# Half of a convolution's taps from VectorE to ScalarE products and GpSimd sums

## The chip, the cores and the metric

The kernel runs on one core of a Trainium2 chip. The core has five engines that work side by side, each with a queue of its own that it takes strictly in order: TensorE (PE in the profile: matrix multiplications, with PEld for the loads of their weights), VectorE (DVE), ScalarE (ACT), GpSimd (POOL) and SyncE (SP, which issues DMAs). An instruction that waits for another engine holds up everything behind it in its own queue. The metric is the device time of one execution in microseconds (us); a comparison is made with the median of several runs.

## The reference, cut to what matters

The program computes three blocks of a network on 512 positions of 1024 features. The change lies in the second block. There a projection of the normalised input yields, among other things, two groups of 1024 columns, `a` and `b`. They make a gated linear unit, and a causal convolution of width 31 runs over the positions, for each feature with its own 31 weights:

```
glu[t, f] = a[t, f] * sigmoid(b[t, f])
z[t, f]   = conv_b[f] + sum over j = 0..30 of conv_w[j, f] * glu[t - 30 + j, f]
z         = layernorm(z) over the features, then silu, times a sigmoid gate
```

In the same block runs a recurrent layer (`rwkv`) over 16 heads. Its state steps depend on each other, chunk after chunk of 64 positions.

## The kernel before, in words

Activations lie with features on the partitions: 1024 features are eight tiles of 128 partitions by 512 positions. Matrix products are made with operands that are split into a high and a low part (three matmuls at L123, L124 and L125 for one product; the text calls these the large matmuls). The weights come by DMA in slabs; ScalarE casts a slab's high part (`whi`, L117) and another engine subtracts to get the low part (`wlo`, L118). In the block in question two slabs of three leave that subtraction to GpSimd (`lo_on = "vpp"`, L1007). The results of the large matmuls lie in four PSUM banks, `psg` (pool `pg`, L37), which are handed out in the order in which the program asks for them: an output that needs a bank waits until whoever reads the bank's earlier content has done so.

The recurrent layer is worked through in eight pairs of heads, 0 to 7. For each pair there are three parts. `rwkv_prep` (L1040) projects to `k`, `r` and `v` by large matmuls of 384 columns, normalises (`ps_kn`, L1086; GpSimd multiplies `kk` at L1104), makes the products `ps_M` (L1117), and writes a piece of them to memory and back in another layout. `rwkv_invert` (L1149) inverts small triangular blocks on VectorE: L1177 is its first instruction, the reductions at L1172 its last; the result goes through memory, and TensorE transposes it (`ps_D`, L1211). `rwkv_steps` (L1232) then makes the eight chunk steps: per chunk TensorE, VectorE (`zV` L1251, `S` L1261) and ScalarE (`zV` L1252, `VU` L1256) hand over to each other several times, and at the end a normalised `Y` is transposed (`ps_yt`, L1281).

The loop at the end of `block2` records, for each pair p, the steps of p, the preparation and inversion of p + 1, and then filler work from the list `order`: `c12` are convolution tiles 1 and 2, `g02` two gate tiles from 0, and so on ("c01", "c12", "c31 g02", "c42", "g22", "c62 g41", ...). Fillers have a lower priority (`fill_offset`). A scheduler puts all of it into the engines' queues when the program is built. What the order in a queue becomes depends on what it expects of each engine.

`conv_tiles` (L1289) makes one convolution tile i: large matmuls for `b` and `a`, ScalarE's sigmoid into `glu` (L1298), VectorE's product with `a` (L1301), ScalarE's tap 0 with the bias into `z[i]` (L1303), and then 30 taps on VectorE, each `z = glu shifted * weight + z` in one instruction (L1305). The first of them is kept behind the last instruction of the inversion that was recorded before (`issue_after`, L1308). GpSimd adds the tile to a running sum `zs` (L1312, L1314). `gate_tiles` (L1322) reads a gate's PSUM bank by a sigmoid into a tile `gs` (L1327) and sends it to memory. That tile comes from the ring `tmp`, which has three buffers:

```
    def tmp(self, name, parts=128):
        return self.sp.tile([parts, T], F32, tag="tmp", name=name, bufs=3)
```

## Time and profile before

| what | value |
|---|---|
| median of 3 runs | 3337.91 us (3335.11 to 3338.43) |
| profiled execution, its own time | 3332.78 us |
| its span in the profile | 3331.0 us |
| granted TensorE clock, mean | 0.983 |
| busy: PE, DVE, ACT, POOL | 95%, 61%, 42%, 15% of the span |
| 240 taps at L1305 | 197.0 us busy, from 1411.2 to 1921.7 us |

A busy TensorE is not TensorE at its peak: matmuls are pipelined and their ends are modelled. Busy shares over the whole program mix stages with different limits, so the stage of the taps has to be read alone. In that stage the text uses the first `ps_D` transpose of each pair as a mark, D0 to D7 for pairs 0 to 7.

### The profile page before, as it was taken

How to read it: one execution, taken by the hardware profiler on the slowest of the kernel's cores; microseconds unless marked ns; L12 is line 12 of the kernel's file. 1: busy time of each engine (PE TensorE's matmuls, PEld its weight loads, DVE VectorE, ACT ScalarE, POOL GpSimd, SP SyncE). 2: the span in 40 equal slices, each digit the busy share in tenths (PEclk: the TensorE clock that was granted, in tenths of full speed). 3: DMA queues.
4: the chain of work that ended last, by engine and by line, in shares of the span. 5: the costliest groups of instructions: out<-in, count | busy, mean ns of one | idle time of the engine just before them, and what ended most of it. 6: DMA issues, size and time to landing. Idle time of an engine off the chain costs nothing. (4 is left out here: it accounts for less than half of the span.)

```text
span 3331.0 us, 43197 instructions
## 1 busy us (share of the span) xinstructions
PE 3179.2 (95%) x15337; PEld 2471.1 (74%) x15337; DVE 2041.3 (61%) x4002; ACT 1386.5 (42%) x2784; POOL 515.1 (15%) x603
## 2 busy tenths in 40 slices
PE   8999999999999999898899889999999999999998
PEld 6755778788778887666666656788877777788887
DVE  4576764654665356688778875434367764575665
ACT  3466332333443233454444444433244553343444
POOL 1000010111211011222223323111010011110111
PEclk9999999999999999999999999999999999999999
DMA  4411553525223332322122343233233125332322
GB/s 134 120 62 50 172 169 128 176 97 149 68 83 95 100 97 76 103 63 68 52 68 66 101 134 113 85 96 95 95 92 112 55 84 164 110 95 95 95 95 82
DMA packets 275032, 332.60 MB, mean 100 GB/s; under 512 B 52956, under 2 KB 188058, under 8 KB 274817
## 3 DMA queue, kind: packets, MB, share of 16 engines
q1 hardware_dynamic: 237392, 301.43, 29.4%
q10 hardware_dynamic: 33489, 12.39, 1.5%
q0 software_dynamic: 3936, 16.03, 1.5%
q8 instruction: 121, 1.98, 0.2%
q14 instruction: 94, 0.77, 0.1%
HBM read 311.88 MB, written 23.89 MB: 101 GB/s over the span
## 5 line engine op out<-in xcount | busy, mean ns | idle before, releaser
L118 DVE TENSOR_TENSOR wlo<-raw,whi 128x512 fp32r<-128x512 f32 (+2 forms) x865 | 625.2, 734 | 752.7 <-PE psg L124 419.3
L123 PE MATMUL psg<-hhi,whi 128*128 128x512 f32 (+1 forms) x2624 | 1044.5, 401 | 36.4 <-DVE glu L1301 7.0
L125 PE MATMUL psg<-hhi,wlo 128*128 128x512 f32 (+1 forms) x2624 | 1038.9, 397 | 13.3 <-DVE wlo L118 7.9
L124 PE MATMUL psg<-hlo,whi 128*128 128x512 f32 (+1 forms) x2624 | 1041.2, 397 | 0.0
L117 ACT CAST whi<-raw 128x512 fp32r<-128x512 f32 (+2 forms) x975 | 581.7, 604 | 1072.6 <-PE psg L124 924.6
L123 PEld LDWEIGHTS psg<-hhi,whi 128*128 128x128 f32 (+1 forms) x2624 | 496.5, 189 | 162.8 <-issue 17.2
L125 PEld LDWEIGHTS psg<-hhi,wlo 128*128 128x128 f32 (+1 forms) x2624 | 496.7, 189 | 124.9 <-POOL wlo L118 9.6
L124 PEld LDWEIGHTS psg<-hlo,whi 128*128 128x128 f32 (+1 forms) x2624 | 497.1, 189 | 107.2 <-issue 7.6
L123 PE MATMUL psg<-hidhi,whi 128*128 128x512 f32 x784 | 308.4, 394 | 1.0 <-DVE ffu L574 0.8
L125 PE MATMUL psg<-hidhi,wlo 128*128 128x512 f32 x784 | 308.0, 393 | 0.0
L124 PE MATMUL psg<-hidlo,whi 128*128 128x512 f32 x784 | 305.9, 390 | 0.0
L1305 DVE SCALAR_TENSOR_TENSOR z<-glu,par_B,z 128x512 f32<-128x512 f32 x240 | 197.0, 835 | 1.5
L118 POOL TENSOR_TENSOR wlo<-raw,whi 128x512 fp32r<-128x512 f32 (+1 forms) x110 | 146.8, 1341 | 281.3 <-ACT whi L117 217.3
L125 PEld LDWEIGHTS psg<-hidhi,wlo 128*128 128x128 f32 x784 | 147.2, 188 | 34.0
L124 PEld LDWEIGHTS psg<-hidlo,whi 128*128 128x128 f32 x784 | 147.2, 188 | 33.4
L123 PEld LDWEIGHTS psg<-hidhi,whi 128*128 128x128 f32 x784 | 147.4, 188 | 32.8 <-DVE ffu L574 1.3
L581 POOL TENSOR_TENSOR ffu<-ffu,ffg 128x512 f32<-128x512 f32 x44 | 64.7, 1469 | 582.6 <-DVE ffu L574 582.6
L1374 POOL TENSOR_TENSOR ffr<-ffr 128x512 f32<-128x512 f32 x32 | 40.1, 1261 | 293.0 <-ACT ffr L1373 286.9
L194 ACT CAST hidhi<-ffu 128x512 fp32r<-128x512 f32 x66 | 41.0, 622 | 106.1 <-POOL ffu L581 66.2
L195 DVE TENSOR_TENSOR hidlo<-ffu,hidhi 128x512 fp32r<-128x512 f32 x66 | 57.3, 868 | 30.9 <-ACT hidhi L194 29.4
L765 DVE SCALAR_TENSOR_TENSOR adacc<-adraw,c_act,adacc 128x1024 f32<-128x1024 f32 x42 | 53.9, 1284 | 33.4 <-DMA adraw<-in_ada_w_dram 33.0
L209 POOL TENSOR_TENSOR ss<-ss,sq 128x512 f32<-128x512 f32 x24 | 35.2, 1467 | 218.1 <-ACT sq L208 202.0
(572 smaller groups left out, 4040.3 us busy)
## 6 DMA issues: line engine op xcount, KB each, us to landing
raw<-in_ffn_w_gu_dram SPq DMA_DIRECT2D x176, 256.0 KB
raw<-in_w_in_dram SPq DMA_DIRECT2D x59, 512.0 KB
adraw<-in_ada_w_dram SPq DMA_DIRECT2D x48, 512.0 KB
raw<-in_w_up_dram SPq DMA_DIRECT2D x88, 256.0 KB
raw<-in_ffn_w_down_dram SPq DMA_DIRECT2D x42, 512.0 KB
raw<-in_w_ff_in_dram SPq DMA_DIRECT2D x32, 512.0 KB
raw<-in_w_ff_out_dram SPq DMA_DIRECT2D x32, 512.0 KB
raw<-in_w_in_dram SPq DMA_DIRECT2D x96, 128.0 KB
```

The costliest lines, as they stand in the source:

```text
L117: nc.scalar.copy(oi(hi), ri(r))
L118: eng.tensor_tensor(out=oi(lo), in0=ri(r), in1=fr(oi(hi)), op=ALU.subtract)
L123: first = nc.tensor.matmul(ps, lhsT=whi, rhs=xhi, start=start, stop=False)
L124: nc.tensor.matmul(ps, lhsT=whi, rhs=xlo, start=False, stop=False)
L125: nc.tensor.matmul(ps, lhsT=wlo, rhs=xhi, start=False, stop=stop)
L194: nc.scalar.copy(hi, t)
L195: nc.vector.tensor_tensor(out=lo, in0=t, in1=fr(hi), op=ALU.subtract)
L209: (nc.gpsimd if c < 4 else nc.vector).tensor_tensor(out=ss, in0=ss, in1=sq, op=ALU.add)
L581: nc.gpsimd.tensor_tensor(out=t, in0=t, in1=part[c], op=ALU.mult)
L765: nc.vector.scalar_tensor_tensor(out=acc, in0=raw, scalar=c[:, k:k + 1], in1=acc, op0=ALU.mult, op1=ALU.add)
L1305: tap = nc.vector.scalar_tensor_tensor(out=z[i], in0=g[:, j:j + T], scalar=cw(j), in1=z[i], op0=ALU.mult, op1=ALU.add)
L1374: nc.gpsimd.tensor_tensor(out=t, in0=t, in1=t, op=ALU.mult)
```

## The change

For the odd tiles (1, 3, 5 and 7) each of the 30 taps becomes two instructions: ScalarE writes `glu` shifted, times the weight, into a new tile of the ring `tmp`, and GpSimd adds that tile to `z[i]`. The even tiles stay as they are. The branch leaves the loop body by `continue`, so for an odd tile nothing is kept behind the inversion.

```diff
             for j in range(1, 31):
+                if i % 2:
+                    pr = self.tmp("tap")
+                    nc.scalar.activation(out=pr, in_=g[:, j:j + T], func=AF.Copy, scale=cw(j))
+                    nc.gpsimd.tensor_tensor(out=z[i], in0=z[i], in1=pr, op=ALU.add)
+                    continue
                 tap = nc.vector.scalar_tensor_tensor(out=z[i], in0=g[:, j:j + T], scalar=cw(j), in1=z[i],
                                                      op0=ALU.mult, op1=ALU.add)
```

Lines behind it move by five: the taps of the even tiles are L1310, the gates L1332. The scheduler now puts the queues together in another order. Three places of it follow, all around tile 3 and the steps of pair 2. In the rows `psg` are the outputs of large matmuls, numbers tell buffers of one name apart.

TensorE before, from the `ps_D` transposes of pair 2 (D2):

```order
L1211 MATMUL ps_D_12768<-ident_81,zD0_10970 128x128 x4
L124 MATMUL psg_13563<-hlo5_10792,whi_13642 128x512
L125 MATMUL psg_13563<-hhi5_10791,wlo_13643 128x512
L123 MATMUL psg_13564<-hhi4_10785,whi_13638 128x512
L1217 MATMUL ps_T_12775<-D_12773,zC_10964 32x32 x16
L124 MATMUL psg_13564<-hlo4_10786,whi_13638 128x512
L125 MATMUL psg_13564<-hhi4_10785,wlo_13639 128x512
L123 MATMUL psg_13564<-hhi5_10791,whi_13642 128x512
L124 MATMUL psg_13564<-hlo5_10792,whi_13642 128x512
L125 MATMUL psg_13564<-hhi5_10791,wlo_13643 128x512
```

TensorE in the change, from the same transposes:

```order
L1211 MATMUL ps_D_12828<-ident_81,zD0_10970 128x128 x4
L1217 MATMUL ps_T_12835<-D_12833,zC_10964 32x32 x16
L1225 MATMUL ps_X_12854<-zD0_10970,zT_10965 32x32 x16
L1253 MATMUL ps_y_13121<-S_13117,ar_12705 64x128
L1255 MATMUL ps_u_13130<-zV0_10968,zD0_10970 64x128
L1259 MATMUL ps_s_13133<-VU_12755,KB_12742 128x128
L1264 MATMUL ps_y_13121<-VU_12755,MLR_12712 64x64 x2
L1248 MATMUL ps_v_13139<-VU_12755,MLR_12712 64x64 x2
L1250 MATMUL ps_v_13139<-S_13117,ar_12705 64x64 x2
L1253 MATMUL ps_y_13121<-S_13117,ar_12705 64x128
L1255 MATMUL ps_u_13147<-zV1_10969,zD0_10970 64x128
L1259 MATMUL ps_s_13150<-VU_12755,KB_12742 128x128
```

Large matmuls stood between the small ones of the inversion's end and of the first steps; now none stands there, and the next one (`psg_13341`, the third output of pair 3's preparation) comes behind chunk 4.

ScalarE before, at the first gate of g02 (`gs_12991`) in the steps of pair 1:

```order
L1256 COPY VU_11915<-ps_u_12299 64x128
L1298 ACTIVATE glu_12885<-psg_12813 128x512
L1327 ACTIVATE gs_12991<-psg_12921 128x512
L1252 COPY zV1_10969<-ps_v_12308 64x64
L1256 COPY VU_11915<-ps_u_12316 64x128
L1268 ACTIVATE Y_12251,gn_m_12252<-ps_y_12290 128x64 x2
L1147 DMA dram_L2_12447<-MLR_12652 32x16x32
L1252 COPY zV0_10968<-ps_v_12328 64x64
```

ScalarE in the change, at the same gates (`gs_13111`, `gs_13114`), with the last products of tile 3 (`tap`), the chunks of pair 2 (`zV`, `VU`) and the casts of pair 3's third slab (`whi_13406`, before it was `whi_13286`):

```order
L1256 COPY VU_12755<-ps_u_13184 64x128
L1307 ACTIVATE tap_13028<-glu_12945,par_B_5986 128x512
L1268 ACTIVATE Y_13119,gn_m_13120<-ps_y_13158 128x64 x2
L1307 ACTIVATE tap_13031<-glu_12945,par_B_5986 128x512
L1307 ACTIVATE tap_13034<-glu_12945,par_B_5986 128x512
L1252 COPY zV0_10968<-ps_v_13196 64x64
L1307 ACTIVATE tap_13037<-glu_12945,par_B_5986 128x512
L1256 COPY VU_12755<-ps_u_13204 64x128
L1332 ACTIVATE gs_13111<-psg_13041 128x512
L1332 ACTIVATE gs_13114<-psg_13042 128x512
L117 CAST whi_13406<-raw_13402 128x384
L1252 COPY zV1_10969<-ps_v_13213 64x64
L117 CAST whi_13410<-raw_13402 128x384
```

The gates and the casts stood in the steps of pair 1 and behind them; now they stand behind the 30th product of tile 3, in the steps of pair 2.

GpSimd before, at the running sum of tiles 0 and 1 and the subtractions for pair 3's weights:

```order
L1312 TENSOR_TENSOR zs_11468<-z0_10980,z1_10981 128x512
L118 TENSOR_TENSOR wlo_13287<-raw_13282,whi_13286 128x384
L1297 MEMSET glu_13705 128x30
L118 TENSOR_TENSOR wlo_13291<-raw_13282,whi_13290 128x384
L118 TENSOR_TENSOR wlo_13321<-raw_13312,whi_13320 128x384
L118 TENSOR_TENSOR wlo_13569<-raw_13565,whi_13568 128x512
```

GpSimd in the change, at the end of tile 3's sums:

```order
L1308 TENSOR_TENSOR z3_10983<-z3_10983,tap_13028 128x512
L1308 TENSOR_TENSOR z3_10983<-z3_10983,tap_13031 128x512
L1308 TENSOR_TENSOR z3_10983<-z3_10983,tap_13034 128x512
L1308 TENSOR_TENSOR z3_10983<-z3_10983,tap_13037 128x512
L1297 MEMSET glu_15305 128x30
L1319 TENSOR_TENSOR zs_11468<-zs_11468,z3_10983 128x512
L118 TENSOR_TENSOR wlo_13407<-raw_13402,whi_13406 128x384
L118 TENSOR_TENSOR wlo_13411<-raw_13402,whi_13410 128x384
L118 TENSOR_TENSOR wlo_13441<-raw_13432,whi_13440 128x384
```

The subtractions for pair 3's later slabs followed the running sum of tiles 0 and 1; now all 30 sums of tile 3 lie between.

## Rows read from the trace of the kernel before

**Rows 1.** The page's part 2, VectorE alone: busy tenths in 40 slices.
```profile
DVE  4576764654665356688778875434367764575665
```

**Rows 2.** Windows D1 to D7: stretch, length; busy us (instructions) per engine; granted clock, DMA share, GB/s.
```profile
1498.89:1589.43 90.54, 81.21 (x495) 59.34 (x494) 75.76 (x163) 40.75 (x106) 26.27 (x31) 0.96 0.24 68
1589.43:1679.08 89.65, 77.03 (x459) 55.97 (x458) 69.05 (x146) 39.47 (x102) 22.10 (x30) 0.90 0.20 53
1679.08:1763.19 84.11, 76.56 (x495) 56.77 (x494) 68.47 (x150) 41.93 (x104) 25.23 (x30) 0.94 0.24 67
1763.19:1841.22 78.03, 69.51 (x433) 49.07 (x432) 64.62 (x144) 38.01 (x103) 25.14 (x30) 0.98 0.28 78
1841.22:1921.83 80.61, 72.91 (x486) 53.67 (x486) 69.32 (x147) 38.51 (x102) 22.66 (x24) 0.98 0.38 104
1921.83:1997.31 75.48, 60.84 (x377) 40.93 (x377) 54.61 (x130) 35.57 (x103) 17.08 (x14) 0.91 0.40 125
```

**Rows 3.** Groups, 1380 to 1950 us: line, engine, operation, shapes, count | busy us, mean ns | idle before.
```profile
L1305 DVE SCALAR_TENSOR_TENSOR z<-glu,par_B,z 128x512 f32<-128x512 f32 x240 | 197.0, 835 | 1.5
...
L118 POOL TENSOR_TENSOR wlo<-raw,whi 128x384 fp32r<-128x384 f32 x44 | 55.5, 1267 | 103.5 <-ACT whi L117 68.7 <-PE psg L125 26.6 <-PE psg L124 3.5
...
L1314 POOL TENSOR_TENSOR zs<-zs,z 128x512 f32<-128x512 f32 x6 | 9.9, 1642 | 9.5 <-DVE z L1305 6.0 <-PE ps_D L1211 3.5
...
L1081 ACT ACTIVATE kk<-xs_k,par_B 128x512 f32<-128x512 f32 x7 | 5.0, 714 | 0.1
```

**Rows 4.** Timeline near 1591 us: start, length, engine, line, operation, tiles [idle before it].
```profile
1590.86 1.27 POOL L1314 TENSOR_TENSOR zs<-zs,z 128x512 f32<-128x512 f32 x1 [2.87 <-DVE z L1305]
...
1591.29 1.39 DVE L1305 SCALAR_TENSOR_TENSOR z<-glu,par_B,z 128x512 f32<-128x512 f32 x1
...
1593.20 0.74 DVE L1305 SCALAR_TENSOR_TENSOR z<-glu,par_B,z 128x512 f32<-128x512 f32 x1
```

**Rows 5.** VectorE's timeline: first and last instruction of the inversions of pairs 0 and 2.
```profile
1391.31 0.29 DVE L1177 COPY uM<-uL 128x256 f32<-128x256 f32 x1 [7.41 <-POOL uL L1161]
...
1409.98 0.67 DVE L1172 TENSOR_REDUCE uX<-uT 128x64 f32<-128x512 f32 x1
...
1537.76 0.37 DVE L1177 COPY uM<-uL 128x256 f32<-128x256 f32 x1 [1.72 <-POOL uL L1161]
...
1577.24 0.71 DVE L1172 TENSOR_REDUCE uX<-uT 128x64 f32<-128x512 f32 x1
```

**Rows 6.** ScalarE's timeline: first gate, pair 3's third slab, chunks 0 and 4 of pair 2.
```profile
1519.28 0.60 ACT L1327 ACTIVATE gs<-psg 128x512 f32<-128x512 f32 x1 [2.92 <-PE psg L125]
...
1551.00 0.52 ACT L117 CAST whi<-raw 128x384 fp32r<-128x384 f32 x1 [0.72 <-PE psg L124]
...
1599.43 0.26 ACT L1256 COPY VU<-ps_u 64x128 f32<-64x128 f32 x1
...
1621.71 0.26 ACT L1256 COPY VU<-ps_u 64x128 f32<-64x128 f32 x1 [0.63 <-PE ps_u L1255]
```

**Rows 7.** TensorE's timeline: `ps_kn` of pair 0, D0, `ps_kn` of pair 3, D2, D3.
```profile
1359.03 1.05 PE L1086 MATMUL ps_kn<-bones,kksq 128*128 128x2 f32 x8
...
1420.49 0.60 PE L1211 MATMUL ps_D<-ident,zD 128*128 128x128 f32 x4
...
1567.94 1.27 PE L1086 MATMUL ps_kn<-bones,kksq 128*128 128x2 f32 x6
...
1589.43 0.60 PE L1211 MATMUL ps_D<-ident,zD 128*128 128x128 f32 x4
...
1679.08 0.60 PE L1211 MATMUL ps_D<-ident,zD 128*128 128x128 f32 x4
```

**Rows 8.** Windows of L123 alone, one in three of the large matmuls (PE, then weight loads).
```profile
1548.90:1589.43 40.53, 16.71 (x39) 7.84 (x39) 0.92 0.29 85
...
2050.00:2100.00 50.00, 26.23 (x68) 12.75 (x68) 1.00 0.33 105
```

**Rows 9.** GpSimd's timeline just behind D3: the product for pair 4.
```profile
1683.98 1.74 POOL L1104 TENSOR_TENSOR kk<-kk,a 128x512 f32<-128x512 f32 x1
```

## Prediction

> **What bounds the kernel now.** I read first the page's forty slices, to find the stage of the taps: they are VectorE's slices 18 to 23, with the digits 8 8 7 7 8 8, the longest high stretch of the program [rows 1]. Then I cut that stage at the first `ps_D` transpose of each pair (L1211). I call these moments D0 to D7, for pairs 0 to 7; between two of them lies one round: the state steps of one pair, the preparation of the next, its inversion, and filler work. The reader is to see three things there. Rounds 1 to 5 last 90.5, 89.7, 84.1, 78.0 and 80.6 us, with VectorE busy for 77 to 86% [rows 2]. The round from D6 has no tap and VectorE is busy for only 54.6 us of it, yet it still lasts 75.5 us [rows 2]. So VectorE is the fullest engine, but most of a round is a chain through five engines, and taking VectorE's work away gives back at most about 10 us of a round. Third, the chain itself: from the `ps_kn` matmul of pair 0 to D0, with no taps on VectorE, 61.5 us pass; for pair 3, with taps, 111.1 us [rows 7]. The inversion is where the difference sits: 19.3 us for pair 0 (1391.31 to 1410.65), 40.2 us for pair 2 (1537.76 to 1577.95) [rows 5].
>
> **The change, part by part.**
> *Removed:* 120 of the 240 taps on VectorE. All 240 take 197.0 us [rows 3], so 98.5 us of VectorE go.
> *Added on ScalarE:* 120 products. The nearest row is L1081, also a scale by a column from SBUF to SBUF at 128x512: 714 ns [rows 3], 86 us in all. ScalarE is busy for 38 to 42 us of each round [rows 2], so the room is there.
> *Added on GpSimd:* 120 sums in place. The same operation stands in L1314: 1.27 us where little runs beside it [rows 4], 1642 ns on average [rows 3]. I take 1.4 us, nearer the lone row, because VectorE will be emptier; 168 us in all, between 152 and 197. GpSimd is busy for 22 to 26 us of a round [rows 2].
> *What VectorE pays:* a tap beside that L1314 takes 1.39 us, and one beside nothing 0.74 us [rows 4]. If every added sum cost VectorE those 0.65 us, 78 of the 98.5 us would be lost again; that is a rival below. The Trainium skill, GPSIMD Engine Reference, § 1 Specifications, says that GpSimd's SBUF interfaces are shared with VectorE, and that VectorE's instructions with two SBUF inputs contend for them. The two taps agree with that rule; by it alone the sum would be that rival's, where by the lone rows it is the forecast's.
>
> The durations matter less than the order. The products use the ring `tmp` of three buffers, so a product waits for the sum three before it, and ScalarE's queue advances at GpSimd's 1.4 us wherever products stand close together. The gates (`gs`, L1327 before, L1332 now) use the same ring.
>
> *Round 1 (D1 to D2): -18 us.* Tile 1's taps leave VectorE, and ScalarE starts z2 only behind tile 1's products, so tile 2's taps now stand behind the inversion of pair 2 (order of VectorE and ScalarE). That inversion falls from 40.2 towards pair 0's 19.3 us: -20 with something for contention. The preparation in front of it is freer too: -5. Against it, eleven of tile 2's taps now stand among the small operations that lead to `Y` of pair 1, and `ps_yt` stands ahead of D2 on TensorE: 11 times 0.74 to 1.39 us, of which the transfer of the inverse covers some: +7. Bounds 0 and -25.
>
> *Round 2 (D2 to D3): +32 us.* This is the term that decides. Before, gate group g02 was read out early (first gate 1519.28) and the cast of the third weight slab of pair 3's preparation stood at 1551.00, during the inversion [rows 6]; TensorE did about 117 of the large matmuls (39 at L123, times three) between 1548.9 and D2 [rows 8]. In the new order the two gates stand behind all 30 products of tile 3, and they hold two of the four `psg` banks; the third output of the preparation needs one of them. On TensorE no large matmul stands from D2 to the state step of chunk 4. So: D2 to chunk 4, as before, 32.3 us (1589.43 to 1621.71) [rows 6, 7]; with four sums in a chunk, 4 x 1.4 = 5.6 us, the pace is the 5.6 us that the chunks have now, so the products cost the steps nothing there. Then two gate reads, a cast and a GpSimd subtraction, 0.6 + 0.6 + 0.5 + 1.3 = 3.0 us [rows 3, 6]; three more chunks, 16.7 us, with 26 of the 60 matmuls that the order has up to `ps_kn` between them; the other 34 at 0.245 us (204 in 50 us [rows 8]), 8.3 us; then the chain from `ps_kn` to D3. I take 61.5 us, pair 0's value, because here too no tap is on VectorE, and about as many large matmuls (147 and 144 by the order) stand on TensorE. Sum 32.3 + 3.0 + 16.7 + 8.3 + 61.5 = 121.8 against 89.65: +32. Lower bound +20, if the last three chunks hide under the matmuls (60 x 0.245 = 14.7 us in place of 16.7 + 8.3). Upper bound +57, if the chain is half way between pair 0's 61.5 and the crowded 111.1 us.
>
> *Round 3: +6 us.* `kk` of pair 4 (L1104), now at 1683.98, five us behind D3 [rows 9], stands behind 26 of tile 5's 30 sums. About nine of them are done by D3; 17 x 1.4 plus six subtractions of 1.4 make 32 us, so the matmuls that use it start some 27 us later in their round. The inversion of pair 4 then has no taps beside it (-19) and waits less in front (-2). Bounds -10 and +20.
>
> *Round 4: 0.* The inversion of pair 5 was done well before D5 already. *Rounds 5 and 6: -8 us.* The inversion of pair 6 loses its taps (-18), but pair 7's preparation is now 34 large matmuls behind D6 (+10).
>
> *What is left over: +18 us.* By D7 the new order has done 90 fewer large matmuls than the old one (74 fewer at the next `ps_yt`). Behind that comes a stretch with a granted clock of 1.00 in which they run at 0.245 us: 74 x 0.245 = 18 us. Bounds 8 (part of it in gaps of the last steps) and 22.
>
> Sum: -18 + 32 + 6 + 0 - 8 + 18 = **+30 us**. On the profiled execution's own 3332.8 us that is 3363; it lay 5.1 us under the median of the three runs (3337.9), so on their scale **3368 us**.
>
> **The rivals.**
> *A, faster: the freed VectorE outweighs round 2.* Four inversions (pairs 2, 3, 4, 6) fall by about 19 us each, and all of it reaches the rounds. Round 1 gives -25, round 2 its lower bound +20, round 3 -10, rounds 5 and 6 -15, and 12 us are left over: -18, 3320 us. For it: VectorE's 77 to 86%. Against it: the round without taps, 75.5 us. It decides at D3: if D3 comes no later than 1679.
> *B, no change:* gains and the loss of round 2 cancel, with half of the leftover hidden: -7 to +7, 3338.
> *C, much slower: contention.* Each sum takes 0.65 us from VectorE and itself needs 1.64 us. Then round 1 and rounds 5 and 6 give nothing (+26), and tile 3's 30 sums outrun the chunks (17 behind chunk 0 by 0.24 us, +4): 3398. For it: the tap of 1.39 us. Against it: 1.27 us for the sum in the same place, and an emptier VectorE. A less busy TensorE can also lose granted clock: it is 0.90 in round 2 and 0.98 in round 4 now [rows 2].
> That the change is not what it says is excluded by the order: 120 taps, 120 products and 120 sums stand there.
>
> **How the numbers follow.** Forecast 0.56, A 0.19, B 0.11, C 0.14. The range: the forecast's bounds without A's and C's extremes are 3340 to 3400; to hold eight in ten I go to 3325 below, short of A's middle, and 3408 above, past C's middle. This kernel's measurement can tell about 0.2%, 7 us, from no change. Faster: A, 0.19; within: B, 0.11; slower: the forecast and C, 0.70.
>
> **What would show it.** D2 some 15 to 20 us earlier than 1589; between D2 and chunk 4 TensorE nearly without large matmuls; gates and casts of pair 3 behind the last product of tile 3; D3 at 1690 or later, with pair 3's `ps_kn` some 60 us behind D2. Inversions of pairs 2, 3, 4 and 6 at 19 to 25 us. Taps on VectorE of 0.75 to 0.9 us, sums of 1.3 to 1.5. I am wrong if D3 is earlier than before, if the chain from `ps_kn` to D3 takes nearer 85 than 62 us, or if the leftover matmuls vanish in gaps.

## The result, and the profile after

The change makes the kernel slower: 3464.32 us (median of 4 runs, 3455.19 to 3465.70) against 3338.12 us of the kernel before beside it, a ratio of 1.0374 (95% interval 1.0356 to 1.0393), or 126 us. The forecast was 3368 us with a range up to 3408: the sign was right, the size four times too small. The profiled execution of after has a span of 3453.4 us against 3331.0, so 122.4 us have to be found in the two traces.

First the page's part 2 of after: VectorE and the granted clock of TensorE in 40 slices [rows 1].

```profile
DVE  4576763654754456757666756543356774575565
...
PEclk9999999999999999996989899999999999999999
```

VectorE's slices 18 to 23, with 8 8 7 7 8 8 before, now have 5 7 6 6 6 7, and TensorE's granted clock, with 9 in every slice of before, dips in the same place (6, 8 and 8). So far this looks as if VectorE had been relieved. The rounds say where the time went. The windows are D0 to D1, and so on to D6 to D7, then D7 to the end of the stage (the first activation of the next block's `ffr`, behind which both kernels run in step, after 122.8 us later); columns as in [rows 2].

```profile
1422.30:1502.60 80.30, 72.59 (x467) 53.68 (x467) 62.75 (x125) 44.10 (x110) 33.56 (x35) 0.96 0.25 67
1502.60:1592.10 89.50, 57.47 (x368) 40.19 (x366) 58.65 (x117) 50.86 (x118) 53.88 (x50) 0.81 0.11 25
1592.10:1718.30 126.20, 92.00 (x499) 67.24 (x500) 74.73 (x130) 65.06 (x143) 74.09 (x68) 0.79 0.17 50
1718.30:1836.00 117.70, 94.41 (x507) 68.57 (x506) 82.87 (x152) 57.85 (x130) 60.06 (x58) 0.84 0.21 61
1836.00:1925.70 89.70, 74.53 (x466) 54.37 (x464) 66.79 (x129) 43.71 (x112) 34.28 (x35) 0.94 0.18 51
1925.70:2005.50 79.80, 57.61 (x369) 41.93 (x370) 45.66 (x93) 44.47 (x111) 44.63 (x40) 0.81 0.23 65
2005.50:2084.30 78.80, 67.70 (x436) 47.73 (x435) 46.73 (x117) 32.81 (x95) 12.98 (x14) 0.94 0.45 132
2084.30:2263.60 179.30, 159.29 (x783) 120.56 (x782) 109.49 (x188) 77.26 (x164) 59.34 (x41) 0.93 0.33 101
```

Against the rounds of before (78.4, then [rows 2]) that is +1.9, -1.0, +36.5, +33.6, +11.7, -0.8 and +3.3 us; D0 itself is 1.8 us later, and behind D7 another 35.4 us are lost. Rounds 1, 2, 3 and 5 have a granted clock of 0.79 to 0.84, where before it was 0.90 to 0.98.

The whole stage in one window each (D0 to the stage's end; before first, then after) is the view that explains most:

```profile
1420.50:2140.80 720.30, 642.36 (x3884) 469.00 (x3883) 549.75 (x1166) 337.96 (x858) 201.00 (x218) 0.95 0.29 82
```

```profile
1422.30:2263.60 841.30, 675.59 (x3884) 494.27 (x3884) 547.67 (x1046) 416.12 (x978) 372.82 (x338) 0.88 0.24 71
```

Two things are to be seen. TensorE has the same 3884 matmuls. Before, it was busy for 642.4 us and idle for 77.9; now it is busy for 675.6 (the same matmuls at a lower clock) and idle for 165.7. So the 121 us of the stage are 88 us of new idle time and 33 us of slower matmuls. TensorE's idle time is what it waits for; three of its longest waits in the stage of after are these (line that waited, who was waited for: us in total, times, longest):

```profile
PE ps_yt L1281 <- ACT Y L1278: 28.1, 13, 6.8
PE ps_v L1248 <- DVE S L1261: 21.6, 9, 7.5
PE psg L125 <- POOL wlo L118: 18.0, 11, 3.9
```

In the stage of before the same three were 3.4, 1.7 and 2.7 us: the first two are the chain of the state steps, the third is GpSimd's subtractions for the weights, which now stand among the sums. ScalarE loads its function tables 15 times in the stage in both kernels, so that is not a part of it.

And VectorE, from which 120 taps were taken, has 120 instructions fewer but is busy for 547.7 us in place of 549.8: it was not relieved at all. The groups show where its gain went (1380 to 2180 us, columns as in [rows 3]):

```profile
L1308 POOL TENSOR_TENSOR z<-z,tap 128x512 f32<-128x512 f32 x120 | 181.4, 1512 | 40.2 <-ACT tap L1307 33.8
L1310 DVE SCALAR_TENSOR_TENSOR z<-glu,par_B,z 128x512 f32<-128x512 f32 x120 | 132.1, 1101 | 3.9 <-ACT z L1303 1.9
L1307 ACT ACTIVATE tap<-glu,par_B 128x512 f32<-128x512 f32 x120 | 83.4, 717 | 28.1 <-POOL z L1308 27.3
```

The remaining taps take 1101 ns in place of 835 [rows 3], and ScalarE's products wait 27.3 us for GpSimd's sums. It is not only the taps. VectorE's timeline in the normalisation of pair 1 (operations of 8 columns, the steps of an inverse square root), and GpSimd's in the same place:

```profile
1576.41 0.16 DVE L254 TENSOR_TENSOR rs_t<-rs_o 128x8 f32<-128x8 f32 x1
...
1577.32 1.85 DVE L1310 SCALAR_TENSOR_TENSOR z<-glu,par_B,z 128x512 f32<-128x512 f32 x1
1579.09 1.25 DVE L256 SCALAR_TENSOR_TENSOR rs_o<-rs_t,rs_o 128x8 f32<-128x8 f32 x1
1580.27 0.74 DVE L1310 SCALAR_TENSOR_TENSOR z<-glu,par_B,z 128x512 f32<-128x512 f32 x1
1580.93 1.24 DVE L254 TENSOR_TENSOR rs_t<-rs_o 128x8 f32<-128x8 f32 x1
```

```profile
1577.33 10.23 POOL L1308 TENSOR_TENSOR z<-z,tap 128x512 f32<-128x512 f32 x6 [2.44 <-ACT tap L1307]
```

Until GpSimd's sums begin at 1577.33, an operation of 8 columns takes 0.16 us; beside them it takes 1.22 to 1.25 us, nearly the length of a sum. The third of the six sums shows how:

```profile
1580.40 1.74 POOL L1308 TENSOR_TENSOR z<-z,tap 128x512 f32<-128x512 f32 x1
```

It ends at 1582.14, and the operation of 8 columns that began inside it, at 1580.93, ends at 1582.17. These operations lie on the chain to `Y` of pair 1. The Trainium skill, SBUF — State Buffer, § Who interferes with whom, says that a VectorE instruction with two SBUF inputs contends with a GpSimd instruction that reads SBUF; it calls the ports that the two share an exclusive lock. The rows agree: what is paid is the rest of the sum, however small the held operation is. Of the 21 operations of 8 columns (L254 to L256, L1276) that begin inside a sum and at least 0.2 us before its end, 20 end 0.02 to 0.03 us behind it. This is a part of the loss and not the whole: over the stage the 131 operations of L254 to L256 take 44.9 us in place of 29.9. In before 9 of them were already held for over 0.9 us, the longest beside GpSimd's subtractions; now it is 20.

What idle time does to TensorE is seen a few microseconds earlier (TensorE's timeline; the gap is the wait for ScalarE's sigmoid `glu`, which stands behind the last products of tile 1 and the squares of pair 1's normalisation in its queue):

```profile
1573.18 0.80 PE L123 MATMUL psg<-hhi,whi 128*128 128x512 f32 x1 [14.22 <-ACT glu L1298]
1573.77 0.63 PE L124 MATMUL psg<-hlo,whi 128*128 128x512 f32 x1
1574.20 0.63 PE L125 MATMUL psg<-hhi,wlo 128*128 128x512 f32 x1
...
1580.33 0.39 PE L124 MATMUL psg<-hlo,whi 128*128 128x512 f32 x1
1580.56 0.39 PE L125 MATMUL psg<-hhi,wlo 128*128 128x512 f32 x1
```

```profile
1570.00:1630.00 60.00, 32.30 (x191) 22.05 (x191) 45.45 (x60) 34.06 (x71) 49.90 (x42) 0.56 0.06 18
```

Behind the gap of 14.2 us the large matmuls follow each other every 0.43 us (the lower level, 1.2 GHz), from 1579 on every 0.23 us. Over the 60 us from 1570 the granted clock is 0.56.

### The profile page after: what moved, and what is told of

Read it like the earlier page. It is cut to its first block, busy times and chain, and to the rows that moved or that the text cites. A ratio compares the mean times of both kernels' runs of the same rounds, so it can differ in the third digit from the quotient of the medians.

```text
span 3453.4 us, 43443 instructions
## 1 busy us (share of the span) xinstructions
PE 3214.6 (93%) x15337; PEld 2498.9 (72%) x15337; DVE 2039.0 (59%) x3882; ACT 1464.6 (42%) x2904; POOL 688.6 (20%) x723
## 5 line engine op out<-in xcount | busy, mean ns | idle before, releaser
L123 PE MATMUL psg<-hhi,whi 128*128 128x512 f32 (+1 forms) x2624 | 1049.4, 402 | 60.3 <-ACT glu L1298 17.5
L123 PEld LDWEIGHTS psg<-hhi,whi 128*128 128x128 f32 (+1 forms) x2624 | 500.1, 191 | 185.8 <-issue 21.3
L123 PE MATMUL psg<-hidhi,whi 128*128 128x512 f32 x784 | 308.7, 394 | 2.1 <-DVE ffu L574 1.1
L1308 POOL TENSOR_TENSOR z<-z,tap 128x512 f32<-128x512 f32 x120 | 181.4, 1512 | 40.2 <-ACT tap L1307 33.8
L123 PEld LDWEIGHTS psg<-hidhi,whi 128*128 128x128 f32 x784 | 147.4, 188 | 34.0 <-DVE ffu L574 1.5
L1310 DVE SCALAR_TENSOR_TENSOR z<-glu,par_B,z 128x512 f32<-128x512 f32 x120 | 132.1, 1101 | 3.9 <-ACT z L1303 1.9
L1307 ACT ACTIVATE tap<-glu,par_B 128x512 f32<-128x512 f32 x120 | 83.4, 717 | 28.1 <-POOL z L1308 27.3
```

The source lines that it names most:

```text
L123: first = nc.tensor.matmul(ps, lhsT=whi, rhs=xhi, start=start, stop=False)
L1307: nc.scalar.activation(out=pr, in_=g[:, j:j + T], func=AF.Copy, scale=cw(j))
L1308: nc.gpsimd.tensor_tensor(out=z[i], in0=z[i], in1=pr, op=ALU.add)
L1310: tap = nc.vector.scalar_tensor_tensor(out=z[i], in0=g[:, j:j + T], scalar=cw(j), in1=z[i], op0=ALU.mult, op1=ALU.add)
```

## Experiments

Two theories stood at the start. ORDER is that of the forecast: the place of the products in ScalarE's queue, and the ring `tmp` that they share with the gates, make the loss. SUMS says that the GpSimd sums make it. SUMS was then split in three: PACE (ScalarE's products wait for the sums through the ring), CONTENTION (VectorE's operations are held while a sum runs) and QUEUE (GpSimd's other work stands behind the sums). All times are medians; a difference is to the kernel before beside it (3337 to 3340 us).

### What emptying VectorE is worth

The odd tiles' taps left out, with nothing in their place:

```diff
                 if i % 2:
-                    pr = self.tmp("tap")
-                    nc.scalar.activation(out=pr, in_=g[:, j:j + T], func=AF.Copy, scale=cw(j))
-                    nc.gpsimd.tensor_tensor(out=z[i], in0=z[i], in1=pr, op=ALU.add)
                     continue
```

> The 120 taps of the odd tiles are left out and nothing takes their place: no product, no sum, 98.5 us less on VectorE; the gates of g02 stand where they stood before the change. This is the most that the change could win. If VectorE's time is on the path as rival A has it: 3290 to 3315 us. If a round is a chain through five engines and VectorE is not the bound: 3320 to 3345 us, within 0.5% of before.

Measured: 3346.53 us, a ratio of 1.0029 (1.0019 to 1.0038): 8.9 us slower than before, with half of the taps gone, and 1.5 us above the range said for a chain. Its windows D0 to D7 and D7 to the stage's end, then those of before:

```profile
1423.50:1973.70 550.20, 482.83 (x3104) 350.88 (x3104) 370.00 (x856) 259.73 (x693) 135.50 (x177) 0.94 0.27 75
1973.70:2151.60 177.90, 158.46 (x782) 120.17 (x781) 109.19 (x191) 77.97 (x165) 57.67 (x41) 0.93 0.32 102
```

```profile
1420.50:1997.30 576.80, 510.73 (x3202) 369.17 (x3200) 470.70 (x1018) 275.65 (x722) 159.83 (x187) 0.95 0.28 78
1997.30:2140.80 143.50, 131.63 (x682) 99.82 (x683) 79.05 (x149) 62.30 (x138) 41.18 (x31) 0.96 0.32 99
```

The rounds do get shorter, by 26.6 us. But 98 matmuls (89 of them large) are then not done in them, and the stretch behind D7 has 100 more and is 34.4 us longer. The rounds are chains with large matmuls as filling; a shorter chain only moves the filling to the end. What counts is TensorE's idle time in the stage, and that is 86.8 us here (728.1 less 641.3) against 77.9. So in the order that the scheduler makes of it, VectorE's 98.5 us are worth nothing by themselves. That no other order could use them is not shown: D3 comes at 1655.0 here, 24 us earlier than before.

The products alone, the sums left out:

```diff
                     nc.scalar.activation(out=pr, in_=g[:, j:j + T], func=AF.Copy, scale=cw(j))
-                    nc.gpsimd.tensor_tensor(out=z[i], in0=z[i], in1=pr, op=ALU.add)
```

> The 120 GpSimd sums are left out (odd tiles keep only tap 0 and the bias); the 120 ScalarE products stay in the ring tmp, and ScalarE's and TensorE's order up to D3 is that of the change (81 large matmuls between D2's neighbours, gates of g02 behind the 30th product of tile 3). Theory ORDER (the place of the products in ScalarE's queue, and what stands behind them, makes the loss): most of the loss stays, 3420 to 3455 us. Theory SUMS (the GpSimd sums make it, by the time they take from VectorE's operations and by holding up GpSimd's other work): the loss goes, 3310 to 3360 us, and VectorE's small operations of 128x8 are at 0.16 us throughout.

Measured: 3382.59 us (1.0138, 1.0122 to 1.0153), +43.7 us. Both theories miss: it lies between. Its rounds are 77.6, 70.5, 112.9, 90.3, 81.4, 76.0 and 78.8 us, that is -0.8, -20.0, +23.2, +6.2, +3.4, -4.6 and +3.3 against before, and +35.0 behind D7. Up to D3 its order on TensorE, ScalarE and VectorE is that of the change, and there the change is 34.9 us longer: that much the sums cost with nothing else changed. Over the whole kernel the products, with the order that comes with them, make 44 of the 126 us (9 of them are there without taps and products), and the sums the other 82.

### What the sums cost

The sums without products (unweighted), no ring, the gates in their old place:

```diff
-                    pr = self.tmp("tap")
-                    nc.scalar.activation(out=pr, in_=g[:, j:j + T], func=AF.Copy, scale=cw(j))
-                    nc.gpsimd.tensor_tensor(out=z[i], in0=z[i], in1=pr, op=ALU.add)
+                    nc.gpsimd.tensor_tensor(out=z[i], in0=z[i], in1=g[:, j:j + T], op=ALU.add)
```

> The 120 products are left out: GpSimd adds the unweighted shifted glu to z in the odd tiles, 120 sums of the same size, no ring tmp, and the gates of g02 stand as early in ScalarE's queue as before the change. Theory ORDER: close to before, 3325 to 3360 us. Theory SUMS: most of the loss stays, 3410 to 3460 us, sums 1.4 to 1.6 us, VectorE's 128x8 operations at 0.8 to 1.2 us where they meet a sum.

Measured: 3423.03 us (1.0258, 1.0243 to 1.0274), +84.1 us, as SUMS expected. With the 43.7 of the products alone the two halves add up to 127.8, near the change's loss, but that they add up is luck. Nothing paces these sums, and the loss lies elsewhere: in rounds 0, 3 and 5 (109.1, 116.8 and 96.5 us in place of 78.4, 84.1 and 80.6), while round 2, the change's worst, is 91.1. TensorE's longest wait is now for GpSimd's subtractions (`wlo`), which stand behind the sums: 55.3 us.

The sums on VectorE:

```diff
-                    nc.gpsimd.tensor_tensor(out=z[i], in0=z[i], in1=pr, op=ALU.add)
+                    nc.vector.tensor_tensor(out=z[i], in0=z[i], in1=pr, op=ALU.add)
```

> Products on ScalarE as in the change, but the 120 sums on VectorE (0.69 us each, 83 us in place of the 90 us of taps before): VectorE's load is back, GpSimd's is that of before. The gates stay behind tile 3's products. Theory ORDER: 3430 to 3480 us, nearly the change's time or above, since VectorE is full again. Theory SUMS: 3335 to 3375 us.

Measured: 3442.07 us (1.0314, 1.0299 to 1.0329), +103.2 us, where ORDER had put it. No GpSimd sum is there. The products idle for 34.8 us, 22.4 of them until a sum on VectorE. So it does not help to take the sums off GpSimd: the products still wait for them through three buffers. (Behind D3 the order is another one, 81 large matmuls in round 3 in place of 193, so what the wait alone costs isn't told by this run.)

The next two take that hand-over away. Here the sums read `glu` and nobody reads the products:

```diff
-                    nc.gpsimd.tensor_tensor(out=z[i], in0=z[i], in1=pr, op=ALU.add)
+                    nc.gpsimd.tensor_tensor(out=z[i], in0=z[i], in1=g[:, j:j + T], op=ALU.add)
```

> Products and sums are both there, but the sums add the unweighted shifted glu and nobody reads the products (left out: the weights of the odd tiles). ScalarE's products no longer wait for GpSimd; ScalarE's and TensorE's order is that of the kernel of products alone (large matmuls between the D marks 172, 81, 204, 179, 166, 118, 140). Theory PACE (the wait of products for sums in ScalarE's queue costs the 82 us between products alone and the change): 3380 to 3400 us. Theory CONTENTION (VectorE held while a sum runs): 3430 to 3465 us, taps at 1.1 us and more. Theory QUEUE (GpSimd's other work behind 30 sums in a row): also 3420 to 3460 us, but with taps at 0.85 us.

And here GpSimd only clears `z`, three times for each sum:

```diff
-                    nc.gpsimd.tensor_tensor(out=z[i], in0=z[i], in1=pr, op=ALU.add)
+                    for _ in range(3):
+                        nc.gpsimd.memset(z[i], 0.0)
```

> As the kernel with unread products, but each sum is replaced by three clears of z (0.53 us each): GpSimd is as long occupied, nothing waits for ScalarE and no two-input operation runs on GpSimd; TensorE's counts between the marks are the change's up to D5. Theory QUEUE: 3420 to 3460 us. Theories PACE and CONTENTION: 3380 to 3405 us. With the one before it, it splits the sums' cost in three.

Measured: 3472.33 us (1.0395, 1.0379 to 1.0410; +132.9) with the sums, 3393.62 us (1.0158, 1.0138 to 1.0179; +54.2) with the clears. The one with sums lies above all three ranges. PACE is in neither. The groups of the one with sums, then of the one with clears (first GpSimd's, then the taps on VectorE; then the 8-column operations of L255 over the stage; last TensorE's wait for GpSimd's subtractions over the stage):

```profile
L1308 POOL TENSOR_TENSOR z<-z,glu 128x512 f32<-128x512 f32 x120 | 169.0, 1408 | 21.0 <-ACT z L1303 13.1
L1310 DVE SCALAR_TENSOR_TENSOR z<-glu,par_B,z 128x512 f32<-128x512 f32 x120 | 121.4, 1012 | 3.7 <-ACT z L1303 2.0
...
L255 DVE TENSOR_TENSOR rs_t<-rs_t,rs_h 128x8 f32<-128x8 f32 x44 | 18.0, 410 | 0.5
...
PE psg L125 <- POOL wlo L118: 44.3, 12, 8.7
```

```profile
L1309 POOL MEMSET z<- 128x512 f32 x360 | 189.2, 525 | 30.3 <-ACT z L1303 13.1
L1311 DVE SCALAR_TENSOR_TENSOR z<-glu,par_B,z 128x512 f32<-128x512 f32 x120 | 98.0, 817 | 3.8 <-ACT z L1303 1.9
...
L255 DVE TENSOR_TENSOR rs_t<-rs_t,rs_h 128x8 f32<-128x8 f32 x44 | 8.3, 191 | 0.6
...
PE psg L125 <- POOL wlo L118: 12.8, 9, 4.8
```

GpSimd is occupied even longer by the clears (189.2 us), yet VectorE's taps take 817 ns in place of 1012 and its small operations 191 in place of 410 (L254 to L256 together: 214 and 383). Occupying GpSimd by clears costs 11 us over the products alone, and sums in their place cost another 79. But these 79 us are not CONTENTION alone. The clears, too, change GpSimd's queue: the subtractions that TensorE needs, and `kk`, cut them into 37 stretches, most of them of at most nine clears, and the sums into 16, one of all 30 sums of a tile. TensorE waits for these subtractions 31.5 us longer beside the sums, which is what QUEUE says. So the pair shows that sums cost far more than clears that occupy GpSimd longer; it does not tell the two theories apart. The two kernels nearly share the order up to D3 (172, 81 and 204 large matmuls in the first three rounds) and differ a little behind it. The Trainium skill, SBUF — State Buffer, § Who interferes with whom, says that a GpSimd instruction that only writes does not contend with two-input operations. Nearly all clears agree: of the 43 operations of 8 columns that begin inside a clear and at least 0.2 us before its end, 40 are not held; three end just behind the clear, after 0.23 to 0.52 us, and why is open.

### In the change's own order

The next three leave TensorE's, ScalarE's and VectorE's queues as they are in the change, word for word, and replace only what stands at L1308: a copy, a scaling and shifting (one input each), and a sum of half the columns.

```diff
-                    nc.gpsimd.tensor_tensor(out=z[i], in0=z[i], in1=pr, op=ALU.add)
+                    nc.gpsimd.tensor_copy(out=z[i], in_=pr)
```

> The change with each sum replaced by a copy of the product into z (left out: the sums of the odd tiles): the same order on every engine word for word, products still wait for GpSimd, but GpSimd reads one tile in place of two. How long the copy takes no trace here shows. If it takes 1.2 us or more and VectorE's taps are back at 0.85 us: theory PACE says 3440 to 3465 us, theory CONTENTION 3385 to 3410. If it takes 0.5 to 0.8 us and the taps are free: both say 3385 to 3410 us. If the taps stay at 1.0 us and more, a one-input copy holds VectorE too, and the time should then be near the change's, 3440 to 3470.

```diff
-                    nc.gpsimd.tensor_tensor(out=z[i], in0=z[i], in1=pr, op=ALU.add)
+                    nc.gpsimd.tensor_scalar(out=z[i], in0=pr, scalar1=1.0, scalar2=0.0, op0=ALU.mult, op1=ALU.add)
```

> The change with each sum replaced by one scaling and shifting of the product into z (one input, two steps; left out: the sums). If this takes 1.2 us or more with VectorE's taps free (0.85 us), it is pace without contention: theory PACE 3435 to 3465 us, theory CONTENTION 3400 to 3415. If it takes as long as the copy, 0.6 to 0.8 us, it should give the copy's time, 3395 to 3412 us, and tells nothing more.

```diff
-                    nc.gpsimd.tensor_tensor(out=z[i], in0=z[i], in1=pr, op=ALU.add)
+                    nc.gpsimd.tensor_tensor(out=z[i][:, 0:256], in0=z[i][:, 0:256], in1=pr[:, 0:256], op=ALU.add)
```

> The change with sums of 256 columns in place of 512 (left out: the second half of each sum), two inputs as before; same order on TensorE, ScalarE and VectorE word for word. A sum should take about 0.65 us beside nothing, no longer than a product (0.72 us), so nothing waits for pace. Theory PACE: like the copy, 3395 to 3410 us. Theory CONTENTION, in proportion to the time that VectorE is held: half of the 60 us stays, 3425 to 3445 us, with taps on VectorE at about 0.95 us on average (0.89 with the copy, 1.10 in the change).

Measured: 3404.00 us for the copy (1.0194, 1.0178 to 1.0209; +64.0), 3401.04 for the scaling (1.0197, 1.0182 to 1.0212; +64.0), 3413.60 for the half sum (1.0236, 1.0219 to 1.0253; +76.6). Groups of the copy, then of the half sum:

```profile
L1310 DVE SCALAR_TENSOR_TENSOR z<-glu,par_B,z 128x512 f32<-128x512 f32 x120 | 104.2, 869 | 3.9 <-ACT z L1303 1.9
L1308 POOL COPY z<-tap 128x512 f32<-128x512 f32 x120 | 96.2, 801 | 50.7 <-ACT tap L1307 46.9
L1307 ACT ACTIVATE tap<-glu,par_B 128x512 f32<-128x512 f32 x120 | 81.6, 715 | 4.4 <-DVE uX L1172 2.1 <-POOL z L1308 1.4
```

```profile
L1308 POOL TENSOR_TENSOR z<-z,tap 128x256 f32<-128x256 f32 x120 | 114.3, 952 | 43.1 <-ACT tap L1307 37.3
L1310 DVE SCALAR_TENSOR_TENSOR z<-glu,par_B,z 128x512 f32<-128x512 f32 x120 | 110.8, 923 | 3.9 <-ACT z L1303 1.9
L1307 ACT ACTIVATE tap<-glu,par_B 128x512 f32<-128x512 f32 x120 | 82.0, 716 | 7.8 <-POOL z L1308 5.5 <-DVE wlo L118 1.1
```

With an operation of 0.80 us behind each product, the products wait only 1.4 us for GpSimd, and 62 of the change's 126 us are gone. The order is the same, so these 62 us are the price of the sum against the copy. It is not split further: the copy holds VectorE as well (all 16 operations of 8 columns that begin inside one, at least 0.2 us before its end, end just behind it), but for 0.46 to 0.61 us, and it is shorter for the products and for GpSimd's other work too. The scaling takes as long as the copy and, as expected for that case, tells nothing more. The half sum has two inputs and takes 0.95 us; it costs only 12.6 us more than the copy, above PACE's range by 4 us and below that of CONTENTION in proportion to length by 11. That could mean PACE, or that holding grows faster than length: both the chance that an operation meets a sum and the time that it then waits grow with it.

To have the pace without the reading, each sum became three clears of the product's buffer:

```diff
-                    nc.gpsimd.tensor_tensor(out=z[i], in0=z[i], in1=pr, op=ALU.add)
+                    for _ in range(3):
+                        nc.gpsimd.memset(pr, 0.0)
```

> The sums are left out and in the place of each GpSimd clears the product's buffer three times (a 128x512 clear took 0.54 us in the trace of before, so 1.6 us a sum, written only, nothing read): GpSimd is held as long and ScalarE's products wait for it through the ring as in the change, but no two-input operation of GpSimd stands beside VectorE's. Theory PACE (ScalarE's queue advances at GpSimd's rate, and GpSimd's other work waits): 3440 to 3475 us, like the change. Theory CONTENTION (VectorE's operations are held while a sum runs): close to the kernel of products alone, 3380 to 3405 us, taps on VectorE back at 0.75 to 0.85 us.

Measured: 3456.07 us (1.0345, 1.0326 to 1.0364), +117.1 us, as PACE expected, with taps of 832 ns and 26.3 us of products waiting for GpSimd:

```profile
L1307 ACT ACTIVATE tap<-glu,par_B 128x512 f32<-128x512 f32 x120 | 84.6, 718 | 33.4 <-POOL tap L1309 26.3 <-POOL uX L1160 4.1 <-DVE z L1311 1.2
```

A kernel with the pace and without the reading thus loses nearly what the change loses. But behind D3 its order is another one (86 large matmuls in round 3, 193 in the change), so only D0 to D3 can be compared, where the order is nearly the same: before 258.6 us, products alone 261.1, copy 266.4. With neither pace nor reading (unpaced clears) it is 267.1, with pace alone (these clears) 284.0, with reading alone (unpaced sums) 305.9, with both (the change) 296.0. So pace costs 16.9 us where GpSimd only writes, and where it reads, the paced kernel is 9.9 us the faster. The two do not add, and no share of either in the change's loss follows. For the rounds behind D3 the split stays open as well: a GpSimd operation with one input and the length of the sum was not found.

### The ring that products and gates share

Products in another ring (two buffers), then gates in another ring, then products alone in another ring:

```diff
-                    pr = self.tmp("tap")
+                    pr = self.sq("tap")
```

> The products take another ring (sq, two buffers) in place of tmp, so the gates no longer wait for a buffer behind them: the first gate of g02 stands about 100 places earlier in ScalarE's queue, and TensorE has 167 large matmuls in round 1 in place of 81. If the tie of products and gates through tmp is what costs round 2 its 36 us, 3410 to 3435 us. Theory SUMS: it stays within 10 us of the change, 3455 to 3475 us. If the order as such matters little, the two-buffer ring may even slow it by some us.

```diff
-            t = self.tmp("gs")
+            t = self.sq("gs")
```

> The products stay in tmp with three buffers, and the gates take the ring sq: a gate then no longer needs a buffer behind the products, though the order still puts the first one only 48 places earlier, with 99 and 175 large matmuls in rounds 1 and 2 (81 and 204 in the change). If the tie through tmp costs round 2: 3425 to 3450 us; the kernel with the products in sq had 3415. If it is the depth of the products' ring that matters: no change, 3455 to 3470.

```diff
-                    pr = self.tmp("tap")
+                    pr = self.sq("tap")
                     nc.scalar.activation(out=pr, in_=g[:, j:j + T], func=AF.Copy, scale=cw(j))
-                    nc.gpsimd.tensor_tensor(out=z[i], in0=z[i], in1=pr, op=ALU.add)
```

> Products alone (sums left out), written into the ring sq in place of tmp, so that no gate needs a buffer behind them; the gates of g02 stand 48 places earlier in ScalarE's queue, TensorE has 99 and 184 large matmuls in rounds 1 and 2 (81 and 204 with tmp). If the tie costs what the forecast gave it: round 2 falls from 112.9 us to about 90, and the time to 3350 to 3368 us. If the loss of round 2 comes from the order alone: 3375 to 3390 us, round 2 above 105.

Measured: 3414.87 us (1.0233, 1.0216 to 1.0250; +75.9), 3444.78 us (1.0313, 1.0296 to 1.0330; +105.4) and 3369.88 us (1.0088, 1.0071 to 1.0105; +29.9), the last 2 us above the range said for the tie. Round 2 falls to 82.3 us with the products moved (126.2 in the change), to 101.7 with the gates moved, and from 112.9 to 91.8 in the kernel of products alone. So the tie is real. Round 2 alone overstates it, since the order moves too: with the products moved TensorE has 167 and 92 large matmuls in rounds 1 and 2, in the change 81 and 204. Rounds 1 and 2 together fall by 31.7, 22.8 and 19.1 us. In all the three moves give back 50, 21 and 14 us. Part of what round 2 gains is lost at once in other rounds: with the products moved, rounds 1 and 3 grow by 12.2 and 9.2 us, and with products alone round 3 grows by 17.6. With the products moved they wait even longer for the sums (40.2 us, two buffers) and VectorE is busy longer (554.5 us in the stage) than in the change, in a kernel that is 50 us faster: neither is a price by itself, what stands behind the waiting work is.

### One tile at a time

```diff
-                if i % 2:
+                if i == 1:
```

and the same with 3, 7 and 5.

> Only tile 1 is changed, the other seven stay on VectorE. Its products and sums lie in the steps of pairs 0 and 1; behind them in ScalarE's queue stand the initialisations and sigmoids of the next tiles, and TensorE has 95 large matmuls in round 1 in place of 196. Theory ORDER: +20 to +45 us over before. Theory SUMS, a quarter of its 82 us: +20 us. If losses need several tiles to meet: within 7 us of before.

> Only tile 3 is changed. The gates of g02 stand behind its 30 products as in the change, and TensorE has 84 large matmuls in round 1 and 214 in round 2. Theory ORDER: it carries the loss of round 2 that was forecast, +30 to +60 us over before. Theory SUMS, a quarter of 82 us: +20 us.

> Only tile 7 is changed; the order up to D4 is that of before word for word, and no gate stands behind its products at once. Theory ORDER: within 10 us of before. Theory SUMS: +15 to +25 us, a quarter of 82 us, since its 30 sums lie beside VectorE's taps of tile 6 and GpSimd's subtractions.

> Only tile 5 is changed. The order up to D3 is that of before; between D3 and D4 TensorE has 57 large matmuls in place of 157, and 288 between D5 and D6 in place of 151. Theory ORDER with SUMS: round 3 and the ones behind it grow by 25 to 55 us, the rounds up to D3 stay within 3 us of before. The singles measured so far are +40 (tile 1), +47 (tile 3) and +18 us (tile 7); if the losses simply add to the change's 126, this one is +21; if it is larger, the tiles overlap.

Measured: tile 1 3379.24 us (+40.3; 1.0118, 1.0103 to 1.0133), tile 3 3386.23 (+47.3; 1.0144, 1.0128 to 1.0160), tile 7 3356.98 (+18.1; 1.0055, 1.0038 to 1.0072), tile 5 3381.53 (+42.1; 1.0125, 1.0110 to 1.0140). They add up to 147.8, more than the change: losses overlap, and no single tile carries them. Tile 5 was expected at +21 if they simply added; the tiles overlap, as the other branch said. Tile 3 alone makes round 2 123.6 us long, with the gates behind its products as in the change. Tile 5 alone loses in round 5 (122.0 us in place of 80.6), where 288 large matmuls stand in place of 151. Tile 7 has the order of before up to D4 and no gate right behind its products; its 18.1 us lie in what SUMS had said, above ORDER's 10. None of the 17 kernels is faster than before, and the fastest is the one without the taps.

## Why the prediction was right or wrong

Each term against the trace of after, and against the kernel of products alone (spans less 3331.0 us):

| term | forecast | after | products alone |
|---|---|---|---|
| D0 and round 0 | 0 | +3.7 | +1.2 |
| round 1 | -18 | -1.0 | -20.0 |
| round 2 | +32 | +36.5 | +23.2 |
| round 3 | +6 | +33.6 | +6.2 |
| round 4 | 0 | +11.7 | +3.4 |
| rounds 5 and 6 | -8 | +2.5 | -1.3 |
| left over behind D7 | +18 | +35.4 | +35.0 |
| sum | +30 | +122.4 | +47.8 |

**What the forecast came near to is the kernel without sums.** But for the last line, it stands within 9 us of the products alone in every round. In round 3 that is luck: the forecast's +6 is made of 27 us behind 17 sums and six subtractions, less 21, and in the kernel without sums `kk` comes 27.5 us behind D3 all the same, since it waits there for VectorE's `ar`. The step that failed is the price of the sums: 1.4 us each on GpSimd, nothing on VectorE, "because VectorE will be emptier". VectorE did not become emptier (549.8 and 547.7 us), a sum took 1.51 us, and the 82 us between the two kernels (74.6 between the two profiled executions of the table) are that step. How much of it is VectorE held, products waiting or GpSimd's subtractions coming late stays open.

**Rival C had the right cause and the wrong sum.** It priced a sum at 0.65 us of VectorE's time. In the stage VectorE is busy for 468.7 us with products alone and 547.7 in the change: 79 us, or 0.66 a sum. But C took this only as gains not made. The held operations are also small ones on the chains, 0.16 us long and then 1.22, where [rows 4] show only large ones; and the products wait for the sums, so the price came on top of the path: 3464, not 3398. Nor is VectorE's time the whole cause: the paced clears leave it at 476.4 us and still lose 117.

**Round 1.** The inversion of pair 2 did fall, as said, from 40.2 to 21.7 us, compare [rows 5]:

```profile
1547.38 1.32 DVE L1177 COPY uM<-uL 128x256 f32<-128x256 f32 x1 [3.20 <-POOL uL L1161]
...
1568.37 0.69 DVE L1172 TENSOR_REDUCE uX<-uT 128x64 f32<-128x512 f32 x1
```

But D2 was then 23 us behind its end, since `ps_yt` of pair 1 stands ahead of it and came at 1588.4, 17.5 us later than before. The forecast had put 7 us on that. The steps of pair 1 took 55.3 us (48.6 before) with the products waiting among them, and the normalisation behind them 30.5 (23.5) with the small operations shown above.

**Round 2** held, part by part (126.2 us; forecast 121.8). Gates and casts of pair 3 stand behind tile 3's products (ScalarE's timeline), and `ps_kn` 57.9 us behind D2 (forecast 60.3), D3 68.3 us behind that (61.5) [rows 6, 7]:

```profile
1625.15 0.72 ACT L1307 ACTIVATE tap<-glu,par_B 128x512 f32<-128x512 f32 x1 [0.39 <-POOL z L1308]
...
1626.50 0.60 ACT L1332 ACTIVATE gs<-psg 128x512 f32<-128x512 f32 x1 [0.34 <-POOL z L1308]
1627.84 0.60 ACT L1332 ACTIVATE gs<-psg 128x512 f32<-128x512 f32 x1 [0.75 <-POOL z L1308]
1628.81 0.51 ACT L117 CAST whi<-raw 128x384 fp32r<-128x384 f32 x1 [0.37 <-PE psg L124]
```

```profile
1592.11 1.11 PE L1211 MATMUL ps_D<-ident,zD 128*128 128x128 f32 x4 [1.21 <-DVE Y L1283]
...
1650.02 1.05 PE L1086 MATMUL ps_kn<-bones,kksq 128*128 128x2 f32 x8 [1.03 <-ACT kksq L1083]
...
1718.27 0.60 PE L1211 MATMUL ps_D<-ident,zD 128*128 128x128 f32 x4
```

The kernel with the products in another ring confirms the tie: 82.3 us. By the forecast's own account this term was to decide, and it did not: it is 37 of 122 us.

**Round 3** had the right wait and the wrong pace. Nine sums of tile 5 were done by D3, as forecast. The 17 behind them, with the subtractions among them, took 2.6 us each and not the 1.9 of the forecast (32 us for 17). The sums themselves took 28.0 us of it (1.65 each), and GpSimd stood idle for 9.4 us, 6.5 of them until VectorE's `xs`, which a small clear in its queue waits for, and 2.8 until a product. So `kk` came 43.6 us behind D3 and not 32 [rows 9]:

```profile
1761.91 1.28 POOL L1104 TENSOR_TENSOR kk<-kk,a 128x512 f32<-128x512 f32 x1
```

That is 12 us of the miss of 28; the chain behind `kk` to the inversion (+5.1 in place of -2), the inversion itself (24.8 us, -13.7 in place of -19) and its way to D4 (+3.5) are the rest.

**Round 4** was taken as 0 because its inversion was long done. It was, 45 us before D5, but D5 waited for `ps_yt` of pair 4, whose normalisation took 36.5 us in place of 22.3 beside the sums of tile 7.

**Rounds 5 and 6** came out 10.5 us above the forecast, and 6.7 of that with the products alone. The inversion of pair 6 did fall (37.5 to 20.7 us); what took its gain back was not followed up.

**The leftover** did not vanish in gaps; it was twice as large, in the products alone too. The 90 matmuls were counted rightly (1059 large ones from D0 to D7 in place of 1149), but 74 of them were priced at 0.245 us each, as in the full stretch, and the 16 that come before the last `ps_yt` at nothing. From D7 to that `ps_yt` it took 66.9 us in place of 53.7, and from there to the stage's end 112.4 in place of 89.8, 0.31 us for each of the 74. With no taps at all, 89 large ones more cost 34.4 us, 0.39 each. And it was booked as one term among others. It is the other side of the gains: what a shorter round leaves undone comes back here.

**Rival A** fell at its own sign, D3 at 1718.3 and not by 1679. The kernel without taps shows what it left out: D3 comes early there (1655.0), and yet the whole is 8.9 us slower, because the large matmuls come back behind D7. **Rival B** fell with the +126 us.

Of the signs: the inversions of pairs 3, 4 and 6 took 18.2, 24.8 and 20.7 us (said: 19 to 25). The taps, said to take 0.75 to 0.9 us, took 1.10; the sums, said 1.3 to 1.5, took 1.51; D2 was not 15 us early but 3 us late. Those three point at the sums: without them the taps took 0.81 us and D2 came 18.8 us early (1570.6).

## What to carry to other kernels

Where TensorE's filling work is fixed, price a change by TensorE's idle time and granted clock over the whole stage; a round that gets shorter gives nothing if its large matmuls move behind it. Before moving work off a busy engine, leave the work out and look at the time: here half the taps gone was worth less than nothing. Before putting work on a third engine, look at what already stands in its queue and who waits for it. Here the products waited 27.3 us for the sums through a ring of three buffers, and the two-input sums on GpSimd took back from VectorE all that the change was to save (549.8 us busy before, 547.7 after).

## What the runs showed of the hardware

- A VectorE operation with two SBUF inputs that began inside a GpSimd sum ended just behind the sum, however small it was: 128x8 in up to 1.25 us in place of 0.16 (20 of 21 in the change, 25 of 25 beside the unpaced sums). Copies with one input held it as well (16 of 16, 0.46 to 0.61 us), clears hardly (3 of 43 beside the unpaced ones, 0 of 21 beside the paced ones).
- On GpSimd a 128x512 sum took 1.26 us at the least in the change (1.09 where it read `glu` in place of a product), one of 128x256 0.72, a 128x512 copy 0.60, a scaling with two steps 0.61, a clear 0.52. The operations with two inputs took about twice as long as those with one.
- The same 3884 matmuls kept TensorE busy for 641 us (no taps) to 676 us (unpaced sums), with granted clocks of 0.94 and 0.87 in the stage: where the stage had more idle time on TensorE (86.8 and 174.9 us), its matmuls were also slower.
